# Adding the down results to the residual in DRAM with accumulating transfers, in a fused encoder block

## The chip, the cores and the metric

One Trainium2 chip, one of its cores. The metric is the device time of one execution of the kernel in microseconds; three runs of the kernel before are given, and their median is what a change is compared with.

## What is computed

The reference is one layer of an encoder trunk on 1024 tokens of width 1024, all in float32: a mixing half, then a SwiGLU half, then a last RMSNorm. The change touches the last matrices of the SwiGLU half:

```
x = x + mix @ w_out                          # residual x, called x1 in the kernel
h = rms_norm(x, ffn_norm_g)
ff = silu(h @ w_gate) * (h @ w_up)           # 1024 x 2816
x = x + ff @ w_down                          # the matrices called "down"
return rms_norm(x, final_norm_g)
```

## The kernel before

Everything is held transposed: features on the 128 partitions, tokens along the free dimension, in two halves of H = 512 tokens. A float32 product is made from two float32r parts of each operand, a high part (a copy on ScalarE, ACT) and a low part (a subtraction on VectorE, DVE), in three passes. `product` is one such product of a 512 x 512 block: 4 blocks of 128 rows by three passes, 12 matmuls, all into one PSUM bank.

The kernel is written in a layer that places waits and buffers by itself and that settles the order of each engine's instructions when the kernel is built; on each engine, and on SP's and GpSimd's queues, that order is then fixed. So the order in the text below is not always that of the trace.

The gate, up and most of the down products are done as Strassen-Winograd products: seven `product`s (named by their weights w1 to w7) give the four blocks of a 2 x 2 block result. Two PSUM banks matter here. X takes w1, then on top of it w6, w7 and w4. Each time, the sum that stands in X after a step belongs to another result block, so X has to be read between one step and the next that adds to it. Z takes w5, then w3; Y takes w2.

The list `seq` holds the matrices in their order: 22 of class `Matrix` (gate and up in turn), then 8 of class `Down`, four for each of two groups of eight feature tiles of ff (`Group`; a group's operands are stored in DRAM by `up_out`, and loaded and split when the group opens). Features 16 to 21 of ff are left to plain products at the end (`down`, line 1084). The main loop (line 1119) does for each matrix m: products 6, 5 and 7 of m, then `first(nxt)` (loads, w1, w2 and `begin` of the next), `rest(nxt)` (sums and the remaining weights of the next), then `end` of m. The two matrices after an opening's first are begun early (`early`).

- Weights of a down matrix come as two raw loads of 512 KB (`load`, tile d_r, two buffers). GpSimd (POOL) forms the sums s1, s2 and s3 from them (lines 836 to 838), ACT and DVE split them (lines 130 and 131).
- Gate and up matrices copy X to an SBUF tile on ACT (lines 828, 863, 868: tiles c11, c12, c22) and add Y or Z to it on DVE (lines 830, 869, 874).
- `Down` instead keeps the residual in the DRAM tensor X1d (8 x 2 tiles of 128 x 512, 256 KB each). For each result block it loads the tile (`acc`, line 999, on SP's queue; tile xa, shown as xad), adds X, Y or Z to it from PSUM on DVE (`add`, line 1007), and stores it (`put`, line 1003, on SP's queue). The last matrix doesn't store: its four tiles are used directly.
- `last_tiles` (line 1096) loads the other twelve tiles of X1d into tiles xf before the last matrix's products.
- After the loop come the loads of the last weights (wdl, two of 512 KB, and wd), the plain products pdl, the addition to xf (line 1232), and the last norm (`finish`).

Of the kernel before, what the change touches and what calls it, by code (L numbers as in the profile page):

```python
# [12 lines left out]
ALU = mybir.AluOpType  # L13
# [7 lines left out]
KT = 8  # L21
# [17 lines left out]
def tile_kernel(ctx: ExitStack, tc: tile.TileContext, xT, wt, wub, wv, wout, wg, wu, wd, wdl,  # L39
                vecs, rows, wsT, out):  # L40
    nc = tc.nc
    PE, ACT, DVE, POOL = nc.tensor, nc.scalar, nc.vector, nc.gpsimd
# [14 lines left out]
    def dt(name, dtype=F32):  # L57
        return dp.tile([P, H], dtype, tag="d", name=name)
# [10 lines left out]
    def mm_ps(name):  # L69
        return pmm.tile([P, H], F32, tag="mm", name=name)  # L70
# [4 lines left out]
    def aux(name):  # L75
        return paux.tile([P, H], F32, tag="aux", name=name)
# [38 lines left out]
    ps = misc("clock")  # L115
# [96 lines left out]
    for hf in range(2):  # L212
        ps = (misc3, aux3)[hf](f"rb{hf}")
# [85 lines left out]
    for c in range(NC):  # L299
        hf, i = divmod(c, NH)  # L300
        ps = mm_ps(f"pu{c}")
# [93 lines left out]
    for c in range(NC):  # L395
        hf, i = divmod(c, NH)
# [21 lines left out]
    for j in range(31):  # L418
        n = 31 - j
# [13 lines left out]
    for c in range(NC):  # L433
        hf, i = divmod(c, NH)
# [8 lines left out]
    for h in range(NH):  # L443
        ps = proj(load_w(wt[12 + h], f"wv_{h}"), f"pv_{h}")
        acc = conv4(conv4_in(ps, f"v{h}"), 8 + h, f"v{h}")
        ACT.activation(acc, acc, AF.Silu)
        for hf in range(2):
# [4 lines left out]
            t = d3(f"vs{h}{hf}")  # L452
# [60 lines left out]
    for c in range(NC):  # L513
        hf, i = divmod(c, NH)
# [81 lines left out]
    for c in range(NC):  # L596
        hf, i = divmod(c, NH)
        ps = mm_ps(f"pv{c}")
# [40 lines left out]
    for h in range(NH):  # L639
        ps = proj(load_w(wt[16 + h], f"wg_{h}"), f"pg_{h}")  # L640
        for hf in range(2):
            t = sg1[:, h] if hf else ft(f"sg{h}")
# [56 lines left out]
    X1d = dram.tile([KT, 2, P, H], F32, name="X1d")  # L699
# [62 lines left out]
    for hf in range(2):  # L762
        acc = ft(f"sqa{hf}")
        n = 0
        for grp in ((3, 1, 1, 1, 1, 1) if hf == 0 else (1,) * KT):
# [7 lines left out]
            if hf == 1 and n == 1:  # L773
                with tc.issue_after(out_mm.last.ins):
                    rh[0] = token_scale(token_sums(sq[0], H, "x0"), H, "x0")
                B11, B21 = (block_h2(n0, b0) for n0 in (0, HB))
# [22 lines left out]
    def product(ps, w, blk, first, last):  # L799
        for k in range(HB):  # L800
            for a, b in PASSES:
                PE.matmul(ps, lhsT=w[a][:, k * P:(k + 1) * P], rhs=blk[b][k], start=(first and k == 0 and a + b == 0),  # L802
                          stop=(last and k == HB - 1 and a == 1), skip_group_check=True)

    class Matrix:
# [54 lines left out]
        def product6(self):  # L860
            product(self.X, self.w6, self.blk["T2"], False, False)
            self.c12 = dt(f"c12{self.name}")
            ACT.copy(self.c12, self.X)
# [16 lines left out]
        def end4(self):  # L880
# [8 lines left out]
    seq = [Matrix(src, pairs[2 * p:2 * p + 2], f"{n}{p}", ffn)  # L889
           for p in range(FT // 2) for src, n in ((wg, "g"), (wu, "u"))]  # L890
# [16 lines left out]
    T1, T2, T4 = (ffn.setdefault(t, [[None] * HB for i in range(2)]) for t in ("T1", "T2", "T4"))  # L907
# [34 lines left out]
    B22 = ffn["B22"] = tiles_b22("")  # L942
# [5 lines left out]
    T3 = ffn["T3"] = tiles_t3("")  # L948
# [38 lines left out]
    class Down(Matrix):  # L987
# [6 lines left out]
        def part(self, i, j):  # L994
            return self.row[j][:, i * H:(i + 1) * H]

        def acc(self, i, hf):
            t = self.x[i, hf] = dt(f"xa{self.name}{i}{hf}")
            nc.sync.dma_start(t, X1d[self.f[i], hf])

        def put(self, i, hf):
            if self is not seq[-1]:
                nc.sync.dma_start(X1d[self.f[i], hf], self.x[i, hf])

        def add(self, i, hf, ps, last=False):
            x = self.x[i, hf]
            DVE.tensor_tensor(x, ps, x, op=ALU.add)  # L1007
            if last:
                self.put(i, hf)

        def begin(self, mid=None):
            n, self.x = self.name, {}
            self.X, Y = mm_ps(f"X{n}"), aux(f"Y{n}")
            self.acc(0, 0)
            product(self.X, self.w1, self.blk["B11"], True, False)
            self.add(0, 0, self.X)
            product(Y, self.w2, self.blk["B21"], True, True)
            self.add(0, 0, Y, True)

        def product6(self):  # L1020
            self.acc(0, 1)
            product(self.X, self.w6, self.blk["T2"], False, False)
            self.add(0, 1, self.X)

        def product7(self):
            for i in range(2):
                self.acc(1, 1 - i)
            product(self.X, self.w7, self.blk["T3"], False, False)
            self.add(1, 1, self.X)
            self.add(1, 1, self.Z, True)  # L1030

        def end(self):
            product(self.X, self.w4, self.blk["T4"], False, True)
            self.add(1, 0, self.X, True)
            product(self.Z, self.w3, self.blk["B22"], False, True)
            self.add(0, 1, self.Z, True)

    class Group:

# [54 lines left out]
    xf = {}  # L1094

    def last_tiles():
        for hf in range(2):
            for i in range(2):
                t = kqp.tile([P, HB, H], F32, tag="kq", name=f"xf{hf}{i}")
                for k in range(HB):  # L1100
                    xf[HB * i + k, hf] = t[:, k]
        for n in range(KT):
            for hf in range(2):
                if n < KT - 2:
                    nc.sync.dma_start(xf[n, hf], X1d[n, hf])

    def open_late(n):
        ps = mm_ps(f"pdl{n}0")
# [10 lines left out]
    for i, m in enumerate(seq):  # L1119
        nxt = seq[i + 1] if i + 1 < len(seq) else None  # L1120
        new, coming = opener.get(i + 1), opener.get(i + 3)
        if coming:
            coming.load("T2", "T1")
        if new:
            new.load("B11", "B21", "T4")
        if nxt is None:
            last_tiles()
        if i > 0:
            m.product6()
            if new:  # L1130
                new.split("B11")
            m.product5()
            if new:
                new.split("B21")
        m.product7()
        if nxt is None:
            for k in range(4):
                split_late(LAST + k, 0)
            wlate = {n: load_w(wd[LAST // 4, n // 2], f"wd{n}") for n in (0, 2)}
            opened = [open_late(0)]  # L1140
        elif i >= 3:
            if new:
                early(seq[i + 2])
                early(seq[i + 3])
            if nxt not in ahead:
                first(nxt)
        if new:
            new.split("T2")
            new.split("T1")
            new.load("T3")  # L1150
        if nxt is not None:
            rest(nxt, i < 3 or nxt in ahead)
        if 0 < i < 3:
            m.product3()
        if i < 3:
            m.end4()
        else:
            m.end()
        if i < FT:
            if i % 2 == 0:  # L1160
                gate_out(m)
                g = m
            else:
                up_out(g, m, i // 2)
        if new:
            new.split("T3")
            new.load("B22")
            new.split("T4")
            new.split("B22")
        if i >= FT and nxt is not None and i + 4 >= len(seq):  # L1170
            for k in (0, 1) if i + 4 == len(seq) else (2, 3) if i + 3 == len(seq) else (4, 5):
                load_late(LAST + k, 0)
    for (n, hf), t in seq[-1].x.items():
        xf[KT - 2 + n, hf] = t
    for k in range(6):
        load_late(LAST + k, 1)
    for k in (4, 5):
# [39 lines left out]
    for c0, c1 in ((0, H), (H, H + H // 2), (H + H // 2, T)):  # L1217
        hf, w = c0 // H, c1 - c0
# [88 lines left out]
```

## Time and profile before

| | |
|---|---|
| time, median of 3 runs | 1175.2 us (1175.12 to 1176.91) |
| profiled execution | 1176.1 us, span 1174.3 us, granted TensorE clock 0.986 in the mean |
| TensorE (PE) busy | 1139.5 us, 97% of the span |
| DVE busy | 796.4 us, 68% |
| ACT busy | 481.6 us, 41% |
| POOL busy | 315.3 us, 27% |
| DMA | 162.66 MB, all on SP's queue but 1 MB of instructions |

The span reaches from the first to the last instruction; 1.8 us of the execution's time lie around it. A busy share is over the whole span, and says little of one stage; matmuls overlap, so that a busy PE is one without gaps, not one at its peak. The granted clock is a share of TensorE's 2.4 GHz; 0.5 is its other level, 1.2 GHz. A line such as L1007 is that of the kernel, PEld is the load of a matmul's weights, and SPq is SP's queue, which issues DMAs in order.

### The profile page before, as it was taken

The page shows a single profiled execution, that of the slowest core. Times are in us where ns is not written, and L with a number is a line of the kernel's source. Part 1 is how long each engine was busy: PE and PEld are TensorE (multiplying, and loading weights), DVE is VectorE, ACT ScalarE, POOL GpSimd, SP SyncE. Part 2 cuts the span into 40 slices and gives each one's busy share as a digit, 9 for nine tenths or more (in the row PEclk, how much of TensorE's full clock was granted, in tenths as well). Part 3 has the DMA queues.
Part 4 walks back from the last instruction along what each step waited for, and adds up shares of the span by engine and source line. Part 5 has one row for each costly group of instructions (what it writes and reads, how often), then busy time and mean ns, then how long its engine had stood idle before and what let it go on. Part 6 is the DMA issues. An engine that isn't in the chain of part 4 may idle for free.

```text
span 1174.3 us, 16040 instructions
## 1 busy us (share of the span) xinstructions
PE 1139.5 (97%) x5878; PEld 939.6 (80%) x5878; DVE 796.4 (68%) x1240; ACT 481.6 (41%) x1007; POOL 315.3 (27%) x244
## 2 busy tenths in 40 slices
PE   8999999999899999979999999999999989989997
PEld 6889888889688778857888888888888867878897
DVE  7699879869987666597545654565445866956523
ACT  7456561224236654454343333333335523523422
POOL 3000140010613221465323232323232232232142
PEclk9999999999999999989999999999999989999998
DMA  6135342463323455313322322232234777678212
GB/s 230 61 95 184 109 127 108 115 208 107 122 71 108 133 181 169 110 54 127 125 93 87 131 94 96 84 135 90 99 126 163 268 258 270 223 251 290 95 68 77
DMA packets 87182, 162.66 MB, mean 139 GB/s; under 512 B 16416, under 2 KB 28352, under 8 KB 87104
## 3 DMA queue, kind: packets, MB, share of 16 engines
q1 hardware_dynamic: 87104, 161.64, 40.5%
q8 instruction: 46, 0.75, 0.3%
q14 instruction: 32, 0.26, 0.1%
HBM read 114.93 MB, written 46.68 MB: 138 GB/s over the span
## 4 chain that ended last, share of the span: by engine, by line
PE 82%; DVE 7%; issue 4%; DMA 3%; POOL 2%; ACT 1%; SPq 0%; POOLq 0%; DVEq 0%; ACTq 0%
PE Xu L802 10%; PE Xg L802 9%; PE po L727 7%; PE Xd L802 7%; PE pdl L1087 5%; PE Zu L802 5%; PE Zg L802 5%; PE pv L228 4%; PE pk L228 3%; PE Zd L802 3%; PE pg L228 2%; PE Yu L802 2%; PE pq L228 2%; PE Yg L802 2%; PE pu L306 2%
## 5 line engine op out<-in xcount | busy, mean ns | idle before, releaser
L664 DVE SCALAR_TENSOR_TENSOR ca<-cy,vec,ca 128x512 f32<-128x512 f32 x120 | 93.1, 798 | 0.4
L131 DVE TENSOR_TENSOR wo_l<-wo_r,wo_h 128x512 fp32r<-128x512 f32 x32 | 27.0, 854 | 24.5 <-ACT wo_h L130 24.4
L836 POOL TENSOR_TENSOR s1d<-d_r 128x512 f32<-128x512 f32 x8 | 10.8, 1352 | 105.9 <-DMA d_r<-in_wd_dram 96.4
L869 DVE TENSOR_TENSOR c22u<-Zu,c22u 128x512 f32<-128x512 f32 x11 | 7.6, 692 | 45.5 <-ACT c22u L868 45.5
L789 POOL TENSOR_TENSOR sqa<-sqa,xr 128x512 f32<-128x512 f32 x13 | 18.1, 1396 | 71.6 <-ACT xr L787 43.9
L1007 DVE TENSOR_TENSOR xad<-Xd,xad 128x512 f32<-128x512 f32 x32 | 21.9, 686 | 22.7 <-PE Xd L802 22.7
L836 POOL TENSOR_TENSOR s1u<-u_r 128x512 f32<-128x512 f32 x11 | 18.8, 1711 | 67.8 <-DMA u_r<-in_wu_dram 67.8
L1241 POOL TENSOR_TENSOR sqf<-sqf,sqt 128x256 f32<-128x256 f32 (+1 forms) x19 | 17.8, 939 | 69.7 <-ACT sqt L1239 68.0
L847 POOL TENSOR_TENSOR s2u<-u_r,s2u 128x512 f32<-128x512 f32 x11 | 18.5, 1679 | 64.1 <-DVE w6u_l L131 64.1
L847 POOL TENSOR_TENSOR s2g<-g_r,s2g 128x512 f32<-128x512 f32 x11 | 18.1, 1641 | 62.5 <-DVE w6g_l L131 62.5
L836 POOL TENSOR_TENSOR s1g<-g_r 128x512 f32<-128x512 f32 x11 | 15.2, 1380 | 67.3 <-DMA g_r<-in_wg_dram 67.3
L130 ACT CAST wo_h<-wo_r 128x512 fp32r<-128x512 f32 x32 | 19.6, 617 | 28.3 <-PE po L727 16.7
L1087 PE MATMUL pdl<-ff_h,wd_h 128*128 128x256 f32 (+1 forms) x96 | 30.9, 322 | 0.0
L1087 PE MATMUL pdl<-ff_h,wd_l 128*128 128x256 f32 (+1 forms) x96 | 30.5, 318 | 0.0
L1087 PE MATMUL pdl<-ff_l,wd_h 128*128 128x256 f32 (+1 forms) x96 | 30.5, 318 | 0.0
L1232 DVE TENSOR_TENSOR xf<-pdl,xf 128x256 f32<-128x256 f32 (+1 forms) x18 | 9.2, 514 | 28.1 <-PE pdl L1087 28.1
L802 PE MATMUL Xg<-b,w1g_h 128*128 128x512 f32 x88 | 27.6, 394 | 0.0
L802 PE MATMUL Yu<-b,w2u_h 128*128 128x512 f32 x88 | 27.6, 394 | 0.0
L802 PE MATMUL Xu<-b,w1u_h 128*128 128x512 f32 x88 | 27.6, 394 | 0.0
L802 PE MATMUL Yg<-b,w2g_h 128*128 128x512 f32 x88 | 27.5, 394 | 0.0
L868 ACT COPY c22g<-Xg 128x512 f32<-128x512 f32 x11 | 6.5, 587 | 48.7 <-PE Xg L802 48.7
L727 PE MATMUL po<-myc_l,wo_h 128*128 128x512 f32 x64 | 25.6, 399 | 0.7 <-DVE myc_l L90 0.7
(581 smaller groups left out, 3949.4 us busy)
## 6 DMA issues: line engine op xcount, KB each, us to landing
u_r<-in_wu_dram SPq DMA_DIRECT2D x24, 512.0 KB, 3.7
d_r<-in_wd_dram SPq DMA_DIRECT2D x24, 512.0 KB, 4.1
g_r<-in_wg_dram SPq DMA_DIRECT2D x23, 512.0 KB, 3.6
wo_r<-in_wout_dram SPq DMA_DIRECT2D x16, 512.0 KB, 3.8
xad<-X1d SPq DMA_DIRECT2D x32, 256.0 KB, 4.2
X1d<-xad SPq DMA_DIRECT2D x28, 256.0 KB, 3.0
FFd<-T SPq DMA_DIRECT2D x24, 256.0 KB, 2.1
xr<-in_xT_dram SPq DMA_DIRECT2D x16, 256.0 KB, 3.6
```

The lines of the kernel that those rows point to most:

```text
L130: ACT.copy(hi, raw)
L131: DVE.tensor_tensor(lo, raw, f32(hi), op=ALU.subtract)
L228: proj.last = PE.matmul(ps[hf], lhsT=cols(wtile, a, kt * P), rhs=(xh, xl)[b][kt][hf], start=(kt == 0 and a + b == 0), stop=(kt == KT - 1 a ...
L306: PE.matmul(ps[:, 0:264], lhsT=a[kt][hf][:, i * P:(i + 1) * P], rhs=b[:, o:o + 264], start=(kt == 0 and a is xh and b is hi), stop=(kt == ...
L664: DVE.scalar_tensor_tensor(o, y(m), w(m), o, op0=ALU.mult, op1=ALU.add)
L727: out_mm.last = PE.matmul(ps, lhsT=cols(wtile, a, kt * P), rhs=mix[hf][kt][b], start=(kt == 0 and a + b == 0), stop=(kt == 3 and a == 1))
L789: POOL.tensor_tensor(acc, acc, xr, op=ALU.add)
L802: PE.matmul(ps, lhsT=w[a][:, k * P:(k + 1) * P], rhs=blk[b][k], start=(first and k == 0 and a + b == 0), stop=(last and k == HB - 1 and a ...
L836: POOL.tensor_tensor(self.s1, a21, a22, op=ALU.add)
L847: (eng or POOL).tensor_tensor(self.s2, self.part(0, 1), self.s2, op=ALU.subtract)
L1007: DVE.tensor_tensor(x, ps, x, op=ALU.add)
L1087: PE.matmul(ps[:, 0:cs.stop - cs.start], lhsT=cols(wtile, a, c), rhs=ff[f, hf][b][:, cs], start=(first and i + a + b == 0), stop=(last and ...
```

## The change

A down matrix forms its four result blocks as a gate matrix does: X is copied to c11, c12 and c22 on ACT, and Y or Z added to them on DVE, through the methods of `Matrix`; the fourth, c21, is a copy of X on ACT. Each finished block is then sent by one DMA on GpSimd's queue that adds it to the tile of X1d in DRAM. The loads and stores of X1d on SP's queue go. The last matrix sends its blocks too, so that `last_tiles` now loads all 16 tiles, and it is called after the loop.

```
-        def acc(self, i, hf):
-            t = self.x[i, hf] = dt(f"xa{self.name}{i}{hf}")
-            nc.sync.dma_start(t, X1d[self.f[i], hf])
-
-        def put(self, i, hf):
-            if self is not seq[-1]:
-                nc.sync.dma_start(X1d[self.f[i], hf], self.x[i, hf])
-
-        def add(self, i, hf, ps, last=False):
-            x = self.x[i, hf]
-            DVE.tensor_tensor(x, ps, x, op=ALU.add)
-            if last:
-                self.put(i, hf)
+        def put(self, i, hf, t):
+            nc.gpsimd.dma_start(X1d[self.f[i], hf], t, accum_op=ALU.add)
 
         def begin(self, mid=None):
-            n, self.x = self.name, {}
-            self.X, Y = mm_ps(f"X{n}"), aux(f"Y{n}")
-            self.acc(0, 0)
-            product(self.X, self.w1, self.blk["B11"], True, False)
-            self.add(0, 0, self.X)
-            product(Y, self.w2, self.blk["B21"], True, True)
-            self.add(0, 0, Y, True)
-
-        def product6(self):
-            self.acc(0, 1)
-            product(self.X, self.w6, self.blk["T2"], False, False)
-            self.add(0, 1, self.X)
+            super().begin(mid)
+            self.put(0, 0, self.c11)
 
         def product7(self):
-            for i in range(2):
-                self.acc(1, 1 - i)
-            product(self.X, self.w7, self.blk["T3"], False, False)
-            self.add(1, 1, self.X)
-            self.add(1, 1, self.Z, True)
+            super().product7()
+            self.put(1, 1, self.c22)
 
         def end(self):
-            product(self.X, self.w4, self.blk["T4"], False, True)
-            self.add(1, 0, self.X, True)
-            product(self.Z, self.w3, self.blk["B22"], False, True)
-            self.add(0, 1, self.Z, True)
+            super().end()
+            c21 = dt(f"c21{self.name}")
+            ACT.copy(c21, self.X)
+            self.put(1, 0, c21)
+            self.put(0, 1, self.c12)
...
         for n in range(KT):
             for hf in range(2):
-                if n < KT - 2:
-                    nc.sync.dma_start(xf[n, hf], X1d[n, hf])
+                nc.sync.dma_start(xf[n, hf], X1d[n, hf])
...
-        if nxt is None:
-            last_tiles()
...
-    for (n, hf), t in seq[-1].x.items():
-        xf[KT - 2 + n, hf] = t
+    last_tiles()
     for k in range(6):
         load_late(LAST + k, 1)
```

## Rows read from the trace of the kernel before

**Rows 1.** Windows: busy time (instructions) by engine, granted clock, DMA share, GB/s
```profile
core 0: us, PE busy (x) PEld busy (x) DVE busy (x) ACT busy (x) POOL busy (x), PEclk, DMA share, GB/s
560.00:917.00 357.00, 357.00 (x1540) 289.20 (x1539) 196.66 (x254) 130.16 (x227) 112.41 (x72) 1.00 0.32 112
917.00:1097.00 180.00, 171.45 (x710) 137.13 (x709) 128.31 (x181) 68.98 (x123) 45.70 (x32) 0.96 0.74 254
```

**Rows 2.** Timeline of PE: start, us, instruction, idle before it and what ended it
```profile
948.72 0.77 PE L802 MATMUL Xd<-T3hT3f,w7d_h 128*128 128x512 f32 x1 [3.77 <-DVE xad L1007]
...
971.80 0.79 PE L802 MATMUL Xd<-T4f0h,w4d_h 128*128 128x512 f32 x1 [1.70 <-DVE xad L1007]
...
1036.46 0.57 PE L802 MATMUL Xd<-T3hT3f,w7d_h 128*128 128x512 f32 x1 [3.08 <-DVE xad L1007]
```

**Rows 3.** Windows right behind the three gaps of PE
```profile
948.70:954.00 5.30, 5.28 (x13) 4.14 (x14) 3.58 (x5) 0.21 (x1) 0.62 (x1) 0.50 1.00 359
...
971.80:976.30 4.50, 4.50 (x13) 3.61 (x14) 1.15 (x2) 0.02 (x1) 0.26 (x1) 0.62 0.57 182
...
1036.40:1040.90 4.50, 4.44 (x13) 3.56 (x14) 3.40 (x5) 0.77 (x3) 0.45 (x1) 0.62 0.53 205
```

**Rows 4.** Timeline of DVE ahead of the first and the third gap's end
```profile
947.29 0.68 DVE L131 TENSOR_TENSOR w6d_l<-s2d,w6d_h 128x512 fp32r<-128x512 f32 x1
947.89 0.68 DVE L1007 TENSOR_TENSOR xad<-Xd,xad 128x512 f32<-128x512 f32 x1
...
1034.02 1.09 DVE L131 TENSOR_TENSOR w6d_l<-s2d,w6d_h 128x512 fp32r<-128x512 f32 x1 [5.44 <-ACT w6d_h L130]
...
1035.64 0.68 DVE L1007 TENSOR_TENSOR xad<-Xd,xad 128x512 f32<-128x512 f32 x1
```

**Rows 5.** Timeline of ACT in the same two places
```profile
945.18 0.62 ACT L130 CAST w6d_h<-s2d 128x512 fp32r<-128x512 f32 x1 [2.25 <-POOL s2d L837]
...
947.78 0.61 ACT L130 CAST w7d_h<-s3d 128x512 fp32r<-128x512 f32 x1
...
1033.37 0.62 ACT L130 CAST w6d_h<-s2d 128x512 fp32r<-128x512 f32 x1 [7.54 <-POOL s2d L837]
```

**Rows 6.** Waits of SP's queue, 916 to 1098 us: total, times, longest
```profile
SPq L1003 <- DVE xad L1007: 48.2, 25, 5.7
```

**Rows 7.** Timelines of SP's queue and POOL ahead of the second gap
```profile
958.97 0.32 SPq L1003 DMA_DIRECT2D X1d<-xad  x1
959.38 0.86 SPq L136 DMA_DIRECT2D d_r<-in_wd_dram  x2
...
964.41 1.28 POOL L836 TENSOR_TENSOR s1d<-d_r 128x512 f32<-128x512 f32 x1 [15.08 <-DMA d_r<-in_wd_dram]
```

**Rows 8.** Instructions by line: ns minimum/median/maximum, first and last start
```profile
L868 ACT COPY c22u<-Xu x11: 585/587/587, 538.4 to 917.2; 128x512 f32<-128x512 f32 x11
...
L1007 DVE TENSOR_TENSOR xad<-Xd,xad x32: 675/691/693, 920.4 to 1094.7; 128x512 f32<-128x512 f32 x32
...
L836 POOL TENSOR_TENSOR s1d<-d_r x8: 1285/1298/1689, 926.6 to 1060.8; 128x512 f32<-128x512 f32 x8
```

**Rows 9.** DMA issues: count, KB each, median us from issue to landing
```profile
d_r<-in_wd_dram SPq DMA_DIRECT2D x24, 512.0 KB, 4.1
...
xad<-X1d SPq DMA_DIRECT2D x32, 256.0 KB, 4.2
X1d<-xad SPq DMA_DIRECT2D x28, 256.0 KB, 3.0
```

**Rows 10.** Timelines of DVE, SP's queue and PE at the end of the last down matrix
```profile
1097.11 0.69 DVE L1007 TENSOR_TENSOR xad<-Zd,xad 128x512 f32<-128x512 f32 x1
...
1097.18 0.33 SPq L136 DMA_DIRECT2D wdl_r<-in_wdl_dram  x1
...
1101.48 1.29 DVE L90 TENSOR_TENSOR wdl_l<-wdl_r,wdl_h 128x512 fp32r<-128x512 f32 x2 [3.08 <-ACT wdl_h L89]
...
1105.30 0.39 PE L1087 MATMUL pdl<-ff_h,wdl_h 128*128 128x512 f32 x1
```

## The prediction, on record before the kernel was run

> **What bounds the kernel now.** I read the page first: TensorE is busy 97% of the span, so only a stage in which it has gaps can give time, and any stage can take some. Then the busy time by windows [rows 1]: from 560 to 917 us, where the gate and up matrices run, PE has no gap at all (357.00 of 357.00 us, 1540 matmuls, 0.232 us each). From 917 to 1097 us, the stage of the down matrices, it is busy 171.45 of 180.00 us, at a granted clock of 0.96. Then the timeline of PE in that stage: the 8.55 us are three gaps, of 3.77, 1.70 and 3.08 us, and all three are ended by the same instruction, the addition of X to a residual tile on DVE at L1007 [rows 2]. They stand in the openings of the two groups (first and third) and once between them. The X bank explains it: the next product adds onto X, so it can't start before DVE has read X out.
>
> Behind each gap PE runs slow: the granted clock is 0.50 over 5.30 us, 0.62 over 4.50 us and 0.62 over 4.50 us [rows 3], where it is 1.00 in the gate stage; 0.50 is the lower of its two levels, 1.2 GHz, and what PE did before each fall was to stand idle. In full-clock time that is 5.30 x 0.50 + 4.50 x 0.38 x 2 = 6.1 us lost. So the stalls of this stage cost about 8.55 + 6.1 = 14.6 us. That is the most that the change can give here, 1.2% of the span.
>
> Why is the addition late? In the fixed order of DVE it stands behind the split of the next matrix's w6 (L131 w6d_l). At the third gap DVE stood idle 5.44 us until ACT had made w6d_h, and the addition came at 1035.64, though PE had finished that X 5 us earlier [rows 4] (between it and the gap lies only the w5 product of 12 matmuls: 1036.46 - 3.08 - 12 x 0.232 = 1030.6 [rows 2]). ACT in turn waited 7.54 us for the sum s2 of POOL [rows 5]. At the second gap the same chain shows its root: POOL waited 15.08 us for the raw load d_r, which SP's queue issued at 959.38, right behind a store of a residual tile at 958.97 [rows 7]. Such stores, each of which waits for its last addition, held SP's queue for 48.2 us in 25 waits [rows 6]. So two things feed the gaps: weights that come late, in part because SP's queue stands behind stores, and a DVE whose order puts the reading of X behind them.
>
> **The change part by part.** *On DVE.* Per matrix seven additions become three. Over 8 matrices 56 go and 24 come, 32 fewer at 0.69 us [rows 8]: 22 us of DVE's 128 us in this stage [rows 1].
>
> *On ACT.* Four copies of X per matrix, 32 at 0.587 us by the same operation in the up matrices [rows 8]: 19 us onto 69 of 180 us [rows 1]. They lie beside other work, except where a copy is what PE waits for, or stands ahead of a late split; for the latter I add 0.6 us in each of the two openings, 1.2 us.
>
> *The gaps.* Where the copy falls in ACT's order decides. Early end: right after X is complete, and the gaps vanish. Late end: behind all of the next matrix's splits; the copy would then start behind w7d_h, 947.78 + 0.61 = 948.39, end at 948.98 [rows 5] and free PE no earlier than the 948.72 of today [rows 2]. I take the place that the addition had on DVE, right behind the w6 split. First gap: 945.18 + 0.62 + 0.59 = 946.39 against PE's start of waiting at 944.95 (948.72 - 3.77): 1.4 us are left. Third: 1033.37 + 0.62 + 0.59 = 1034.58 against 1033.38: 1.2 us. Second: no opening, ACT is free there, 0. So 2.6 of 8.55 us stay. The slow clock: the smallest gap seen, 1.70 us, already cost 4.50 x 0.38 = 1.7 us; for two gaps below it I take half, 1.7 us of the 6.1. Gain: 14.6 - 2.6 - 1.7 = 10.3 us.
>
> *On SP's queue.* 32 loads, 28 stores and their waits go, four loads come at the end. The loads of d_r can then be issued when their buffer is free and not when a store behind a DVE addition has left. This makes s1, s2 and w6 earlier, by up to some us; I count it only as cover for the next cost.
>
> *On POOL.* 32 DMAs are issued from a queue on which this trace has none. Lower bound: what SP takes for an issue, 0.33 us [rows 10]. Upper bound: the longest sum on POOL, 1.69 us. I take the sum's median, 1.3 us [rows 8], since it is POOL itself that works. In all 42 us (11 to 54) onto 45.7 of 180: no bound by throughput. But the queue is in order: what is behind a put is the next matrix's s1 and s2, and behind these are w6's split, the copy of X, and PE. A put that waits for its block holds them. The sums are ready when d_r has landed, before the blocks of the same matrix exist, so I expect them ahead of its puts; only the puts of the matrix before can stand ahead. I take one put of 1.3 us in each of the two openings: 2.6 us, 0 if SP's relief covers it.
>
> A put may also slow DVE. While POOL summed, the w6 split at 1034.02 took 1.09 us, against 0.68 us for the one at 947.29 [rows 4]; if each put stretched one split so, that would be 32 x 0.4 = 13 us of DVE, less than the 22 us it is rid of; on the path I count one stretched split in each opening, 0.8 us (0 to 13). The Trainium skill (SBUF — State Buffer, Who interferes with whom) has it that a DVE addition or subtraction with two SBUF inputs collides with a GpSimd instruction that reads SBUF, and infers that issuing a DMA is not such a case. By that page the 0.8 us are 0 and the sum below is -6.5; no row here has a put to show it, so I keep the row's price.
>
> *The transfers.* An accumulate reads and writes X1d, so its landing lies between that of a store, 3.0 us, and that of a load and a store, 4.2 + 3.0 = 7.2 us [rows 9]; for the DMA engines it is at most what the load and the store were, at a DMA share of 0.74 [rows 1]. Nobody waits for it but the tile's buffer, and at the end `last_tiles`.
>
> *The end.* Tiles 6 and 7 are now loaded after the last puts. The last block is complete at 1097.80; put, landing and load take at most 1.3 + 7.2 + 4.2 = 12.7 us, to 1110.5. Tile 6 is added to after the plain products of tiles 0 to 6, from 1105.30 on 4 x 6 + 3 x 18 matmuls at 0.232 us, at 1123.4: hidden. What could hurt is what stands behind these loads on SP's queue. The load of the last wdl weights left at 1097.18, while the last addition to Z ran [rows 10], so it doesn't wait for that block, and I take it that it stays ahead of a load that does: 0.
>
> Sum: -10.3 + 1.2 + 2.6 + 0.8 = -5.7 us on the profiled 1176.1 us (span 1174.3 and 1.8 us around it), 1170.4 us; that execution lies 0.9 us above the median of 1175.2, so the median comes to 1169.5 us.
>
> **The rivals.** *The order keeps the stall.* The copies of X end up behind the splits on ACT as the additions did on DVE (the late end above). For it: ACT too waits on late sums. Against: SP's relief moves the sums. The gaps stay, ACT and POOL costs are hidden: 1174 to 1177 us.
>
> *POOL becomes the late link* (the other side). Two puts stand ahead of s1 where d_r is late, as it was at the second gap [rows 7]; at 1.3 to 1.69 us each the chain to the copy of X ends 2.6 to 3.4 us later at each of the three gaps. For it: queue order is fixed, and there are four puts for four sums per matrix. It decides when a put and its wait hold s1 longer than SP's relief and the quicker copy bring it forward, 1 to 4 us. With nothing won by SP: 7.8 to 10.2 us, less the 3 x 0.69 us of the shorter DVE chain: 6 to 8 us, 1181 to 1183 us. The Trainium skill (SBUF — State Buffer, its box on "DVE blocks DMA") gives a GpSimd-issued DMA about 3.1 us instead of 0.62 beside a DVE copy that locks the shared port; at 3.1 us a put this rival would cost about twice as much. The page excepts the two-input additions that fill DVE here, and no row here can show either.
>
> *The tail waits.* The last weight load, issued at 1097.18, falls behind the load of the tile whose put comes last. That block is added by 1097.80, put by 1099.1, landed 3.0 to 7.2 us after; the weights, ready at 1102.77 today and needed at 1105.30 [rows 10], would be 4.9 to 9.1 us later: a stall of 2.4 to 6.6 us, and 1.7 to 2.7 us of slow clock. On top of the gain of 5.7: 1174 to 1179 us.
>
> **How the numbers follow.** The forecast (gaps mostly gone) has 0.52, its own range 1160.6 (all 14.6 us, nothing paid) to 1172.8 (just measurable); the stall kept 0.20; POOL late 0.15; the tail 0.13. About 0.2% (2.4 us) is what a measurement of this kernel can tell from no change. The stall kept is faster, same, slower by 0.06, 0.12, 0.02; the tail by 0.05, 0.04, 0.04; POOL late is slower by 0.15. Faster 0.63, same 0.16, slower 0.21. The range of 8 in 10 is 1161 to 1181: it leaves out half of POOL late, and some of the forecast's far end.
>
> **What would show it.** Right: in the down stage the gaps that DVE ended at L1007 are gone or under 1.5 us and the waits of SP's queue on L1007 with them; d_r lands sooner; PE's clock stays at 1.00. Wrong: PE waits on an ACT copy for as long as it did on DVE (stall kept); s1 on POOL follows a put or a long wait (POOL late); PE has a gap before 1105 us at the first wdl product (tail). A new order of all engines may also open a gap in a place that has none now, which no row can tell.

## The result, and the profile after

The changed kernel took 1193.65 us (median of 4 runs, 1192.44 to 1197.35), the kernel before 1175.16 us on the same chip: a ratio of 1.0156, 95% interval 1.0139 to 1.0173. It is 18.5 us slower; 1169.5 was forecast, and the range ended at 1181. The profiled execution took 1192.44 us, its span 1190.6.

From the timelines of PE I cut both spans at the same products (first w1 product of a down matrix, last w3 product of one, first product with wdl):

| stretch | before, us | after, us | difference |
|---|---|---|---|
| up to the first down product | 917.0 | 914.9 | -2.1 |
| down matrices | 180.1 | 189.9 | +9.8 |
| from there to the first wdl product | 8.2 | 14.2 | +6.0 |
| the rest | 69.0 | 71.5 | +2.5 |

The first row is not put down to the change, which starts behind it: in the other kernels below the first down product starts between 915.3 and 920.1 us.

Windows of the changed kernel (stretch; busy time and instructions of PE, PEld, DVE, ACT, POOL; granted clock, DMA share, GB/s): down stage, the stretch to the first wdl product, and the 12 matmuls behind that.

```profile
914.90:1104.90 190.00, 174.62 (x710) 136.19 (x709) 103.97 (x138) 78.61 (x142) 76.63 (x62) 0.96 0.70 192
1104.90:1119.10 14.20, 8.36 (x37) 6.40 (x35) 7.03 (x11) 6.96 (x13) 1.76 (x2) 0.94 0.81 223
...
1119.09:1124.20 5.11, 5.11 (x12) 4.05 (x13) 3.33 (x6) 1.81 (x4) 0.00 (x0) 0.50 0.45 162
```

DVE went from 128 to 104 us, as counted. ACT went from 69 to 79 us where 19 more were counted: 31 of the 32 copies lie in the stage, but 12 splits of late weights and of ff now fall behind it. Yet PE now stands idle 15.4 of 190 us where it was 8.55 of 180, at the same granted clock of 0.96 [rows 1]. What it waits for, 900 to 1140 us (total, times, longest):

```profile
PE pdl L1064 <- ACT wdl_h L89: 5.8, 1, 5.8
PE Xd L802 <- DVE w6d_l L131: 5.1, 3, 2.7
PE Xd L802 <- ACT c12d L863: 3.9, 2, 2.7
PE Xd L802 <- ACT c22d L868: 3.7, 5, 1.0
PE Xd L802 <- ACT w6d_h L130: 1.5, 3, 1.1
PE Yd L802 <- ACT w2d_h L130: 1.2, 1, 1.2
```

The three gaps that the additions ended [rows 2] are gone. In their place there are the first w6 products of both openings, and one between them, which wait for their weights; one wait for w2; two waits for the copy of X; five short ones where w4 now follows w7 directly (in the kernel before, matmuls with the next matrix's w6 stood between them at four such places: the layer settled another order for PE too); and one long one at the tail.

*Why w6 is late.* POOL of the changed kernel from the first down product on:

```profile
921.72 1.03 POOL L998 DMA_DIRECT2D X1d<-c11d  x1 [19.71 <-DVE c11d L830]
927.87 0.87 POOL L998 DMA_DIRECT2D X1d<-c11d  x1 [5.12 <-DVE c11d L830]
932.98 0.86 POOL L998 DMA_DIRECT2D X1d<-c11d  x1 [4.24 <-DVE c11d L830]
933.54 1.62 POOL L836 TENSOR_TENSOR s1d<-d_r 128x512 f32<-128x512 f32 x1
...
947.60 5.16 POOL L836 TENSOR_TENSOR s1d<-d_r 128x512 f32<-128x512 f32 x1 [4.95 <-DMA d_r<-in_wd_dram]
```

and the same sum in the kernel before:

```profile
926.62 1.36 POOL L836 TENSOR_TENSOR s1d<-d_r 128x512 f32<-128x512 f32 x1 [22.56 <-DMA d_r<-in_wd_dram]
```

Three matrices are begun at an opening, and the puts of all three c11 stand ahead of the first one's s1. A put takes 0.86 us; what costs is its wait for a block that PE and DVE still have to finish. So s1 starts 6.9 us later.

The late sums reach PE mostly by way of DVE. They now run beside the four subtractions that make T1f0l, which stand ahead of w6's split in DVE's order. The changed kernel, and `e1` of the next section, which has the same order and no puts, so that its three sums are over by 930.7:

```profile
933.20 6.52 DVE L1044 TENSOR_TENSOR T1f0l<-T1f0l,T1f0h 128x512 fp32r<-128x512 f32 x4
```

```profile
933.58 2.49 DVE L1044 TENSOR_TENSOR T1f0l<-T1f0l,T1f0h 128x512 fp32r<-128x512 f32 x4
```

The 4.0 us between them are more than the 2.67 us that PE waits for w6d_l there. In the second opening it is the same: 6.52 us against 2.49, and a wait of 2.06 us. Of the kernels below, those with the c11 puts on POOL ahead of the sums (e3, e6, e9, e11), and e7 with what stands in for them, have 6.2 to 6.5 us in both openings, and those with the sums ahead (e1, e2, e4, e12, e14, e15) have 2.5.

*The tail.* SP's queue, two of its waits (916 to 1120 us: total, times, longest), and the product that waits for it:

```profile
1104.57 0.33 SPq L1081 DMA_DIRECT2D xf<-X1d  x1
1104.95 2.98 SPq L1056 DMA_DIRECT2D fr<-FLd  x5
1114.50 0.32 SPq L1081 DMA_DIRECT2D xf<-X1d  x1
1114.92 0.38 SPq L1056 DMA_DIRECT2D fr<-FLd  x1
1115.39 0.38 SPq L136 DMA_DIRECT2D wdl_r<-in_wdl_dram  x1
```

```profile
SPq L1081 <- DMA X1d<-c21d: 6.5, 1, 6.5
SPq L1081 <- DMA X1d<-c22d: 5.9, 1, 5.9
```

```profile
1119.09 0.80 PE L1064 MATMUL pdl<-ff_h,wdl_h 128*128 128x512 f32 x1 [5.84 <-ACT wdl_h L89]
```

The loads of tiles 6 and 7 wait in the queue until the puts have landed, and the last raw tile and the last weights stand behind them: 1115.39 instead of 1097.18 [rows 10]. The put of c21 leaves late itself, at 1107.28: its copy stands on ACT behind a split of wd that waited 7.62 us for its load.

### The profile page after: what moved, and what is told of

It is laid out like the page before. It is cut to its first block, busy times and chain, and to the rows that moved or that the text cites. A ratio compares the mean times of both kernels' runs of the same rounds, so it can differ in the third digit from the quotient of the medians.

```text
span 1190.6 us, 16010 instructions
## 1 busy us (share of the span) xinstructions
PE 1143.0 (96%) x5878; PEld 938.5 (79%) x5878; DVE 781.5 (66%) x1208; ACT 498.3 (42%) x1039; POOL 346.7 (29%) x276
## 3 DMA queue, kind: packets, MB, share of 16 engines
q0 software_dynamic: 4608, 8.39, 4.2%
## 4 chain that ended last, share of the span: by engine, by line
PE 74%; issue 8%; DVE 6%; POOL 5%; DMA 4%; ACT 2%; SPq 0%; POOLq 0%; DVEq 0%; ACTq 0%
PE Xu L802 10%; PE Xg L802 9%; PE po L727 7%; PE Zu L802 5%; PE pdl L1064 5%; PE Zg L802 4%; PE pv L228 4%; PE pq L228 4%; PE pk L228 3%; PE pg L228 2%; PE Yu L802 2%; PE Yg L802 2%; PE pu L306 2%; PE pv L603 2%; PE Xd L802 2%
## 5 line engine op out<-in xcount | busy, mean ns | idle before, releaser
L847 POOL TENSOR_TENSOR s2u<-u_r,s2u 128x512 f32<-128x512 f32 x11 | 18.5, 1681 | 61.8 <-DVE w6u_l L131 61.8
L1205 DVE TENSOR_TENSOR xf<-pdl,xf 128x256 f32<-128x256 f32 (+1 forms) x24 | 12.3, 513 | 35.8 <-PE pdl L1064 35.7
L868 ACT COPY c22u<-Xu 128x512 f32<-128x512 f32 x11 | 6.5, 588 | 46.9 <-PE Xu L802 46.9
L727 PE MATMUL po<-myc_h,wo_h 128*128 128x512 f32 x64 | 25.5, 398 | 0.0
```

The lines of the kernel that those rows point to most:

```text
L727: out_mm.last = PE.matmul(ps, lhsT=cols(wtile, a, kt * P), rhs=mix[hf][kt][b], start=(kt == 0 and a + b == 0), stop=(kt == 3 and a == 1))
L847: (eng or POOL).tensor_tensor(self.s2, self.part(0, 1), self.s2, op=ALU.subtract)
```

## The experiments

All are edits of the changed kernel, unless they say of the kernel before; the times are medians of 4 to 12 runs, the ratio is to the kernel before, measured beside it (its median there 1175.4 to 1176.2 us). "Stage" is the length of the down matrices in the profiled execution, as in the table above (180.1 before, 189.9 after). It is that of one execution: most lie within 2.4 us of their kernel's median, but those of e2 and e3 5.2 and 4.7 us below it and that of e14 3.8 us above, so stages that differ by 2 or 3 us are not told apart.

**No puts, and two mends of order.** `e1` leaves the put out. `e2` moves c11's put behind the sums:

```
-            self.put(0, 0, self.c11)            # in begin
+        def sums(self):
+            super().sums()
+            with tc.issue_after(self.last_sum): # s3
+                self.put(0, 0, self.c11)
```

`e3` gives the last matrix the methods of the class before, with its own residual tiles (`class Last(Down)`, acc and add as before), so that `last_tiles` stands ahead of it again. `e4` has both.

> The 32 accumulating transfers are left out and nothing takes their place: the down results of the first 20 feature tiles never reach the residual. Theory Q1 (the puts do the harm: in POOL's order they hold the sums s1 and s2 of each opening, and at the end the loads of the residual wait for them on SP's queue): in the changed kernel the first opening loses 5.9 us and the second 4.4 us at the w6 product, the tail 5.84 us of gap and 2.5 us of slow clock, 18.6 us in all; without puts 1193.7 - 18.6 = 1175 us, with no gap before the first wdl product and s1 in the openings right behind its load. Rival Q2 (reading X by ACT copies is itself worse than by DVE additions, puts or not): only the tail goes, 1193.7 - 8.3 = 1185 us, and the w6 products of the openings stay late.

> Only the order on POOL changes: each put of c11 is issued behind the three sums of its own matrix, not ahead of them. Q1: the w6 products of both openings come in time, 5.9 + 4.4 = 10.3 us less, 1183 us, and the tail's gap of 5.84 us stays. If the puts of c22 and c12 of the matrix before are as much to blame, less than half of that. Q2 (the ACT copies): no change, 1193 us.

> The last down matrix alone is as before the change: its residual tiles are loaded, added to on DVE and kept, and the other twelve tiles are loaded ahead of its products. Q1: SP's queue waits for no put at the end, the last weights come in time, 5.84 us of gap and 2.5 us of slow clock go: 1193.7 - 8.3 = 1185 us. Rival (the last weights are late because the stage before them ends late and the DMA queues are full, whatever the puts): the gap before the first wdl product stays at 4 us or more, 1190 us or more.

> The two edits before together: puts of c11 behind the sums, and the last matrix as before the change. Q1: both savings add, 1193.7 - 10.3 - 8.3 = 1175 us, level with the kernel before. If one cause feeds the other (a later stage makes the tail late), the sum is less than the parts: 1178 to 1184 us. Q2: 1185 us.

| run | us | ratio, 95% interval | stage | to wdl |
|---|---|---|---|---|
| e1_no_put | 1170.30 | 0.9955, 0.994 to 0.9969 | 174.6 | 8.2 |
| e2_puts_after_sums | 1191.88 | 1.0134, 1.0104 to 1.0164 | 185.7 | 12.6 |
| e3_last_kept | 1190.49 | 1.0134, 1.0116 to 1.0151 | 191.3 | 8.0 |
| e4_both | 1188.74 | 1.0104, 1.0068 to 1.014 | 192.1 | 8.0 |

The puts cost 23.4 us; without them the change is 4.9 us faster than the kernel before (by the ratio 5.3), and lies below both expectations. That gain is clock: PE still waits 8.1 us in the stage of e1, but its granted clock is 1.00 (with the stretch to wdl):

```profile
916.00:1097.00 181.00, 172.91 (x738) 137.76 (x737) 104.77 (x151) 85.79 (x157) 50.73 (x32) 1.00 0.51 173
```

The two mends did remove the waits that they aimed at (w6 in e2, the tail in e3), but won only 1.8 and 3.2 us, and the intervals of both overlap that of the changed kernel. In e2 PE waits for the copy of X behind product 6 instead:

```profile
PE Xd L802 <- ACT c12d L863: 10.1, 4, 3.8
```

and in e3 the last matrix waits 3.2 us for its residual. e4 is slower than all three expectations for it. That the two mends together give back what the puts cost is refuted.

**Transfer, queue and order, separately.**

```
-            nc.gpsimd.dma_start(X1d[self.f[i], hf], t, accum_op=ALU.add)
+            nc.sync.dma_start(X1d[self.f[i], hf], t)             # e5
+            nc.gpsimd.dma_start(X1d[self.f[i], hf], t)           # e6
+            POOL.tensor_tensor(j[:, 0:320], t[:, 0:320], t[:, 0:320], op=ALU.add)  # e7, j a scratch tile
+            nc.gpsimd.dma_start(X1d[self.f[i], hf, :, 0:H // 2], t[:, 0:H // 2], accum_op=ALU.add)  # e9
```

> The blocks overwrite the residual tiles by plain stores on SP's queue (the residual of these tiles is left out of the sum). No puts first was 1170.3 us. Theory R1 (what is left of the harm after reordering is POOL's queue: time and waits ahead of the sums): without POOL the stage of the down matrices is again under 177 us (174.6 without puts), and only stores that hold SP's queue cost something, 1171 to 1178 us. Theory R2 (the harm is traffic: whatever carries the blocks delays the loads of weights): 1180 us or more.

> The same plain stores, issued on POOL's queue at the places of the accumulating ones (the residual of these tiles is left out of the sum). R1 (POOL's queue): as slow as the changed kernel, 1188 to 1194 us, since POOL's order, issue time and waits are the same. R2 (traffic): a plain transfer takes the DMA engines half of what an accumulating one does (by the profiles 0.78 us against 1.56 us of all 16 for 256 KB), so about half of the 23 us that the puts cost is left: 1180 to 1184 us.

> No put is made; in its place POOL adds a block's first 320 columns to themselves into a scrap tile, which waits for the block as the put did and takes about the 0.87 us of a put (the residual lacks the blocks). No traffic, same queue order. R1: the w6 products of both openings are late as in the changed kernel and the stage of the down matrices takes 185 us or more; the tail has no wait, so 1180 to 1185 us in all. R2: 1170 to 1173 us, as without puts.

> The changed kernel, but each put takes only columns 0 to 255 of its block: as many puts at the same places of POOL's queue, half the bytes (the residual's right halves are left unchanged by the down matrices). POOL's order alone cost 7.7 us (1177.97 against 1170.30), the accumulating transfers another 15.7 us (1193.65 against 1177.97). If what costs is the bytes, half of the latter goes: about 1186 us. If it is the number of puts and the place of each in the queue, the time stays within 3 us of 1193.65.

| run | us | ratio, 95% interval | stage | to wdl |
|---|---|---|---|---|
| e5_plain_sp | 1181.06 | 1.0041, 1.0019 to 1.0063 | 186.0 | 8.3 |
| e6_plain_pool | 1187.46 | 1.0101, 1.0072 to 1.0129 | 186.6 | 10.0 |
| e7_pool_busy | 1177.97 | 1.0024, 1.0009 to 1.004 | 182.3 | 8.2 |
| e9_half_put | 1188.73 | 1.0102, 1.0079 to 1.0124 | 186.3 | 14.0 |

On SP's queue (e5) the transfers leave POOL alone, yet the stage is as long as with e6: PE waits 9.0 us in three gaps for the copy of c12, which stands behind the next matrix's splits on ACT. But e5 does not show traffic alone: the stores hold SP's queue 98.5 us in waits for their blocks, and the layer settled another order. Plain puts on POOL (e6) cost 6.2 us less in all than accumulating ones, of it some 4 at the tail, where the gap is 1.6 us.

Between e1, e7, e6, e9 and the changed kernel the traces have the same order of instructions on every engine and queue in this stage, up to the loads of `last_tiles` at its end and leaving aside the puts and what stands in for them. So these five differ there in POOL's waits and in the transfers alone, and not in order. PE stands idle 8.1 us in the stage of e1, 10.3 in e7's and 15.4 in the changed kernel's, at a granted clock of 1.00, 0.97 and 0.96.

e7 has the waits of POOL and no transfer: 7.7 us over e1, in both totals and stages, with w6 late in both openings as in the changed kernel. It is no exact copy of the puts' order: what stands in for a put took 0.72 to 1.18 us where a put took 0.85 to 1.03, and DVE was busy 112.8 us in the stage against 104.0. The accumulating transfers add 15.7 us to that. In the stage half of the bytes cost about half, within what one execution each can tell: 182.3, 186.3, 189.9. Plain puts of all the bytes cost the stage as much (186.6) as accumulating ones of half; queue 0 kept the DMA engines busy 1.8% of the span there and 2.5% in e9, against 4.2% in the changed kernel. R1 (the queue) and R2 (the traffic) each hold in part: e6 and e7 fall between the two ranges. The tail doesn't depend on the bytes (14.0 and 14.2): there it is the landing of the last put that the queue waits for. This is why e9's total lies nearer to the changed kernel than the 1186 us of a cost by bytes alone.

How the bytes cost time is seen behind the first opening, where these three kernels issue the same loads in the same order: eight of a group's operands between two of d_r. Issues with count, KB, median us to landing, for e7 (953 to 976 us), e9 (950 to 975) and the changed kernel (953 to 974):

```profile
d_r<-in_wd_dram SPq DMA_DIRECT2D x4, 512.0 KB, 3.6
T2f1l<-FFd SPq DMA_DIRECT2D x4, 256.0 KB, 4.3
T1f1l<-FFd SPq DMA_DIRECT2D x4, 256.0 KB, 5.3
```

```profile
d_r<-in_wd_dram SPq DMA_DIRECT2D x3, 512.0 KB, 4.0
T2f1l<-FFd SPq DMA_DIRECT2D x4, 256.0 KB, 5.3
T1f1l<-FFd SPq DMA_DIRECT2D x4, 256.0 KB, 6.9
...
```

```profile
d_r<-in_wd_dram SPq DMA_DIRECT2D x2, 512.0 KB, 6.4
T2f1l<-FFd SPq DMA_DIRECT2D x4, 256.0 KB, 6.4
T1f1l<-FFd SPq DMA_DIRECT2D x4, 256.0 KB, 9.3
X1d<-c22d POOLq DMA_DIRECT2D x1, 256.0 KB, 6.4
X1d<-c21d POOLq DMA_DIRECT2D x1, 256.0 KB, 7.2
X1d<-c12d POOLq DMA_DIRECT2D x1, 256.0 KB, 8.0
```

Operands and weights land later from kernel to kernel, as more bytes are put beside them.

**Forming and traffic.** `e8` forms the blocks as gate's, but loads and stores the residual on SP as before, added on DVE from SBUF. `e10` is the kernel before without that traffic:

```
+            x = self.x[i, hf]; DVE.tensor_tensor(x, t, x, op=ALU.add)     # e8, in put
+            nc.sync.dma_start(X1d[self.f[i], hf], x)
-            nc.sync.dma_start(t, X1d[self.f[i], hf])                      # e10, in acc; put: pass
-            DVE.tensor_tensor(x, ps, x, op=ALU.add)
+            DVE.tensor_tensor(x, ps, y, op=ALU.add)   # y: first time a tile of the right operand
```

> The residual tiles are loaded and stored on SP's queue as before the change, and the blocks are formed as gate's are; a fourth addition per matrix and block, from SBUF on DVE, brings the two together, and the last matrix keeps its tiles. It has the ACT copies alone, and no put. If it is the reading of X on ACT that gave the 5 us without puts, it keeps them, less what 21 us more of DVE cost: 1168 to 1174 us. If the 5 us came from the transfers that were gone, it is level with the kernel before or slower, 1175 to 1182 us.

> The kernel before, without its 28 loads and 28 stores of residual tiles in the first seven down matrices; DVE makes the same additions, the first of each block with a tile of the right operand in place of the residual (so the residual is left out). If the 4.9 us that the changed kernel without puts has over the kernel before come from forming the blocks as gate's (fewer DVE operations, X read by ACT), this kernel stays at 1175 us, within 2 us. If they come from transfers and SP waits that are gone, it comes to 1170 us, and forming the blocks as gate's has won nothing.

e8: 1181.78 us, ratio 1.0062 (1.0043 to 1.008), stage 186.0: with the residual's traffic kept, and a fourth addition per block and another order with it, the new forming of the blocks wins nothing; SP's queue waits 73.4 us in 27 stores for DVE (48.2 in 25 before [rows 6]), and PE 5.1 us for c12. e10: 1185.09 us, 1.0071 (1.0051 to 1.0092), stage 188.5. Neither theory had e10 slower than before. The layer had settled a different order: the addition of X stands far behind splits now, and PE waits for it 17.6 us in six gaps, of which the longest is

```profile
953.61 0.76 PE L802 MATMUL Xd<-T3hT3f,w7d_h 128*128 128x512 f32 x1 [8.97 <-DVE xad L1010]
```

So e10 says nothing on what the traffic costs; it shows that an edit that takes away transfers and an operand can lose 9 us with the order that comes with it. What gave e1 its 4.9 us, the forming or the traffic that is gone, stays open.

**The tail by its queue.**

```
-                nc.sync.dma_start(xf[n, hf], X1d[n, hf])
+                nc.gpsimd.dma_start(xf[n, hf], X1d[n, hf])
```

> The changed kernel with the 16 loads of last_tiles on GpSimd's queue, behind the puts they wait for, so that SP's queue no longer waits for puts at the end. If the wait of SP's queue held the last weights back, the gap of 5.84 us ahead of the first wdl product goes and the slow clock behind it: 8.3 us less, 1185 us, with the down stage as it was (189.9 us). If the weights come late for their buffer or for the transfers, the gap stays and the time within 2 us of 1193.65.

> The changed kernel with both mends that leave the arithmetic as it is: the put of c11 behind the sums of its own matrix, and the loads of last_tiles on GpSimd's queue. If the two places cost separately, 4 us of the down stage and 8 us of the tail go: 1182 us. If the late weights of the transfers take over what is freed, it stays at 1186 to 1190 us. In neither case is it below the 1175.2 us of the kernel before.

e11: 1185.43 us, ratio 1.0075 (1.0055 to 1.0095); 8.2 us less than the changed kernel, as expected of the queue's wait, stage 189.3, and to wdl 8.2. SP's queue and the product:

```profile
1108.72 0.33 SPq L136 DMA_DIRECT2D wdl_r<-in_wdl_dram  x1
```

```profile
1115.59 0.39 PE L1064 MATMUL pdl<-ff_h,wdl_h 128*128 128x512 f32 x1
```

The tail is settled: it was SP's queue behind loads that wait for puts. e12, with e2's order as well: 1184.75 us, 1.0071 (1.005 to 1.0092), between the two expectations, but only 0.7 us better than e11; PE waits 9.4 us for c12.

**The place of the read of X.** The copy of X stood behind splits on ACT in e2, e5 and e12 as the addition did on DVE before. Three kernels force it ahead: `e13` is the kernel before, `e14` is e12 and `e15` is e1 with

```
+            if i in opener:
+                with tc.issue_after(m.read):      # the read of X behind product 6
+                    opener[i].split("T4"); opener[i].split("B22")   # from the opening before
-            rest(nxt, i < 3 or nxt in ahead)
+            with tc.issue_after(m.read):          # m a down matrix
+                rest(nxt, nxt in ahead)
```

and `e16` is e13 with the splits of B22 behind the first addition of product 7.

> The kernel before, with one order forced: the splits of the next matrix (on DVE), and at an opening those of T4 and B22, stand behind the first addition of X after product 6. Arithmetic and transfers are as before. If the stall is the place of that addition in DVE's order, the gaps of 3.77 and 3.08 us and the slow clock behind them go: 9 to 13 us less, 1162 to 1167 us. If the weights that come late (d_r, the sums) are the cause, TensorE waits for the next w6 instead and the time stays within 3 us of 1175.2.

> The changed kernel with the two mends of e12_order_xf (1184.75 us) and the same order forced on ACT: the copy of X behind product 6 ahead of the splits of the next matrix and of T4 and B22. TensorE's waits for that copy were 9.4 us in four gaps there, with some 4 us of slow clock behind them. If the copy's place is the cause they go: 1171 to 1175 us. If late weights are, the wait moves to the split of w6 and the time stays at 1182 to 1187 us.

> The changed kernel without its puts (the down products are left out of the residual), 1170.3 us, with the order of e14_x_first. Without transfers weights are early; TensorE's waits for the copy of c12 there were 3.5 us in two gaps. If the copy's place is the cause: 1165 to 1167 us. If not: 1169 to 1172 us.

> e13_before_x_first with the splits of B22 behind the first addition of product 7. If that gap is of the order alone, it and its slow clock go in both openings (2.93 and 1.71 us, and about 1.7 us of clock each): 1163 to 1167 us. If the splits of B22 are then late for w3, the gap moves to w3 and the time stays at 1169 to 1172 us.

| run | us | ratio, 95% interval | stage |
|---|---|---|---|
| e13_before_x_first | 1170.32 | 0.9952, 0.9935 to 0.9969 | 176.8 |
| e14_x_first | 1187.74 | 1.0107, 1.0084 to 1.0129 | 195.1 |
| e15_no_put_x_first | 1169.80 | 0.995, 0.9931 to 0.9969 | 174.1 |
| e16_before_b22_later | 1174.57 | 0.9986, 0.9972 to 1.0 | 177.2 |

With the transfers on SP the place of the read was a cause: e13 gains 5.2 us, beats both kernels, and is the best of those that leave nothing out. It missed the 1162 to 1167 us, since the gap ahead of w7 came back ahead of w4, where the addition stands behind the splits of B22:

```profile
947.49 2.49 DVE L1069 TENSOR_TENSOR B22B22f<-B22B22f,B22B22f 128x512 fp32r<-128x512 f32 x4
949.89 0.68 DVE L1007 TENSOR_TENSOR xad<-Xd,xad 128x512 f32<-128x512 f32 x1
```

```profile
950.63 0.52 PE L802 MATMUL Xd<-T4f0h,w4d_h 128*128 128x512 f32 x1 [2.93 <-DVE xad L1007]
```

Holding these back too (e16) moved it again, to w6 and w4 (1.90 and 2.14 us), and the time came out above both expectations. Without transfers the place cost nothing that shows: in e15 the waits for c12 went, one of 2.98 us for c22's addition came ahead of w3, and the time is within 0.5 us of e1. With the puts the theory fell: in e14 two of the four waits for c12 went, the others grew to 3.5 and 5.9 us, and a late w6 came to them. In this stage e14 differs from e12, and e15 from e1, in ACT's order alone. Its timelines of PE, ACT, POOL and SP's queue:

```profile
975.54 0.80 PE L802 MATMUL Xd<-T2f0h,w6d_h 128*128 128x512 f32 x1 [5.74 <-ACT w6d_h L130]
```

```profile
974.86 0.62 ACT L130 CAST w6d_h<-s2d 128x512 fp32r<-128x512 f32 x1 [10.97 <-POOL s2d L837]
```

```profile
946.51 5.43 POOL L836 TENSOR_TENSOR s1d<-d_r 128x512 f32<-128x512 f32 x1 [4.32 <-DMA d_r<-in_wd_dram]
...
972.24 1.25 POOL L836 TENSOR_TENSOR s1d<-d_r 128x512 f32<-128x512 f32 x1 [11.11 <-DMA d_r<-in_wd_dram]
```

```profile
954.59 0.33 SPq L136 DMA_DIRECT2D d_r<-in_wd_dram  x1
954.98 2.19 SPq L1039 DMA_DIRECT2D T2f1l<-FFd  x4
957.21 2.23 SPq L1039 DMA_DIRECT2D T1f1l<-FFd  x4
959.72 20.91 SPq L136 DMA_DIRECT2D d_r<-in_wd_dram  x3
```

Read backwards: w6's split waits for a sum, the sum for a d_r that is issued at 959.72 behind eight operand loads; these stand behind a d_r that waits for a raw buffer, which POOL frees with s3, after a sum of 5.43 us (beside DVE's splits of T4 and B22). Then four puts and eight loads are in flight at once.

## Why the prediction was wrong

*The forecast gain* (10.3 us). The mechanism is there and its size was half: without puts the stage is 5.5 us shorter (e1). I took the gain to be 6 us of gaps and 4 us of clock; it is nearly all clock. The gaps that went were replaced by others as long in sum, among them five of 0.67 to 0.96 us where PE's new order has w4 behind w7 with nothing between, and these short ones left the granted clock at 1.00. So did the two of 1.73 and 1.78 us for c12, though the kernel before lost 1.7 us of clock behind one of 1.70 [rows 3]: the prediction's price of a gap by its length does not carry over. That PE's order would change is only in the prediction's last sentence, without a price.

*The step that failed first*: "The sums are ready when d_r has landed, before the blocks of the same matrix exist, so I expect them ahead of its puts; only the puts of the matrix before can stand ahead." In both openings the puts of three begun matrices stand ahead, and they hold POOL not for the 1.3 us of an issue (it is 0.86) but until the last of the three blocks is made. The forecast had 2.6 us for it; the price is 7.7 us (e7 against e1). I had named late POOL as a rival, at 7.8 to 10.2 us before what the shorter DVE chain gives back. That this is near 7.7 is luck: it counted two issues at each of three gaps, and what came is a wait in two openings, which DVE passed on.

*SP's relief.* The stores' waits of 48.2 us [rows 6] did go. But the loads of d_r also wait for the buffers that POOL's s3 frees, and that wait grew. SP's queue, 916 to 1120 us, in the kernel before and in the changed one:

```profile
SPq L136 <- POOL s3d L838: 12.2, 5, 5.8
```

```profile
SPq L136 <- POOL s3d L838: 68.9, 7, 14.8
```

Not all of it hurts: without puts it is 42.8 us, and that kernel is the faster one. But POOL now stands in a loop (d_r, sums, the buffer, the next d_r) with the puts inside it; I had looked at each queue by itself.

*The transfers*, priced at 0, since they take the DMA engines no longer than the loads and stores that go. That bound may hold (below), and the conclusion from it doesn't: in the stage they cost another 7.6 us (189.9 against 182.3 for the same order on POOL), with the same order on every engine; they are in flight when the weights and the next group's operands are loaded, and these land later. (The puts themselves landed in 3.7 to 8.5 us, half of them within 6.3; the bounds were 3.0 and 7.2.)

*The tail*, priced at 0 with "I take it that it stays ahead of a load that does" wait. It does not stay ahead: 8.2 us (e11), of it 5.8 of gap and 2.5 of slow clock. The rival had 2.4 to 6.6 and 1.7 to 2.7 us: right in kind and size.

*A split stretched by a put* (0.8 us): no put stretched one, but the row behind this price, a split that took 1.09 us while POOL summed [rows 4], was the mechanism of the late w6. The puts moved the sums beside DVE's subtractions, which took 4.0 us longer in each opening. I had priced what a put does to DVE, and not what it does by moving the sums. Two sums on POOL were stretched too, to 5.16 and 3.38 us from a median of 1.62; the copy of X ahead of a late split (1.2 us) can't be told apart from the order.

The rivals were added up as if one excluded the others. Late POOL and the tail came true together, and with the transfers they are the sum: -5.5 + 7.7 + 7.6 in the stage, +6.0 and +2.5 behind it, -2.1 ahead of it: 16.2 us, against 16.3 between the spans. These are differences of stretches, which add up by themselves; what the experiments add is the cause of each but the last, which is how executions differ. What isn't settled is what part of the 7.7 belongs to e7's stand-in, and which of the late landings make up the 7.6. Nor did any mend bring the stage back: each kernel with transfers on GpSimd's queue kept one of 186 to 195 us.

## What to carry to other kernels

Before a DMA moves to a compute engine's queue, write down what its issue waits for, what stands behind it there, and what that work will run beside when it is late: the wait, not the issue, was the price here, and the loads whose buffers that engine frees wait with it. A stall that one instruction ends may be a matter of order: forcing that order in the old kernel (e13) gave as much as the whole rewrite gave without its transfers (e15), though in the rewrite itself it gave nothing (e14). And rivals that sit in different places add up.

## What the runs showed of the hardware

An accumulate took the DMA engines longer than a plain store. Queue 0 carries only puts; its packets, MB and share of 16 engines' span in the changed kernel and in e6 (plain stores of the same bytes), with queue 1 of the changed kernel:

```profile
q1 hardware_dynamic: 79040, 146.96, 36.8%
q0 software_dynamic: 4608, 8.39, 4.2%
```

```profile
q0 software_dynamic: 2560, 8.39, 1.8%
```

Per byte that is 2.3 times a plain store of the same queue, and twice the mean of queue 1 (4.2 / 8.39 = 0.50% per MB against 0.25%), about as much as a load and a store together.

The 5.16 us sum of POOL ran while DVE made eight subtractions with two SBUF inputs in a row:

```profile
946.73 2.48 DVE L1044 TENSOR_TENSOR T4f0l<-T4f0l,T4f0h 128x512 fp32r<-128x512 f32 x4
949.14 2.48 DVE L1044 TENSOR_TENSOR B22B22f<-B22B22f,B22B22f 128x512 fp32r<-128x512 f32 x4
```

DVE kept its 0.62 us each, and POOL's sum ended 1.1 us after the last. In the openings it was the other way round: there DVE's four subtractions took 6.52 us, and POOL's three sums beside them 1.62 to 1.73 each. The Trainium skill (SBUF — State Buffer, Who interferes with whom) has it that a DVE instruction with two SBUF inputs contends with a GpSimd instruction that reads SBUF; this trace agrees, with 5.16 us for a sum that took 1.69 in the kernel before (at 941.76), and 6.52 us for subtractions that took 2.49 in e1. It also infers that issuing a DMA is not such a case: the 32 puts of the changed kernel took 0.85 to 1.03 us each, whatever DVE did, which agrees too. In e14 eleven of the 32 took 1.17 to 1.55 us, all with another instruction of POOL in flight, so that run can't tell.
